# A hybrid attention and DeltaNet layer on one core: later transfers of weight sums, another queue for the reloads of y, and plain stores for the last results

## The chip, the core and the metric

The kernel runs on one core of a Trainium2 chip. A core has five engines with instruction lists of their own: TensorE (PE, matmuls; its weight loads are listed as PEld), VectorE (DVE), ScalarE (ACT), GpSimd (POOL) and SyncE (SP). They meet only at semaphores. Transfers between the chip's memory (DRAM) and the core's SBUF are issued from the list of SP or of GpSimd and are moved by 16 DMA engines. An engine works through its list in order, so what stands behind a waiting instruction waits too.

The metric is the device time of one execution in microseconds. Where a single execution is looked at, it is one that the profiler recorded.

## The reference, cut to what matters

One decoder layer for 512 positions (T) and width 2048 (D), all in float32:

```python
h = rms_norm(x, norm_w) * (1.0 + scale) + shift        # scale, shift, gate from c
proj = h @ w_in
y_a = (swa_attention(aq, ak, av, sinks) * silu(ag)) @ w_o_swa
o = gated_delta_rule(dq, dk, dv, g, beta)              # 32 heads, chunks of 64
y_b = (rms_norm(o, dn_norm_w) * silu(dz)) @ w_o_dn
y = sigmoid(mg_a) * y_a + sigmoid(mg_b) * y_b
return x + gate * (y @ w_out)
```

The change concerns the last line: `y @ w_out`, the gate, and the addition of x.

## The kernel before, in words

A float32 product is made of three matmuls on halves of a number: `split` (line 50) casts a tile to a high part on ACT (line 52, `whi`) and subtracts to get the low part on DVE (line 53, `wlo`), and `mm3` (line 237) issues the three matmuls, lines 240 to 242. Every weight tile of 1 MB is loaded by SP into one of two `raw` buffers (`load_job`, line 195), split in two halves into one of three pairs of `whi` and `wlo`, and used by PE. `channel_tile` (line 244) is one tile of 128 channels: 48 matmuls of 512 columns. After each second step of eight it calls `pump` (line 81), so 8 times a tile. `pump` does the weight work that is due, moves on the live chains of the heads, and moves on the side jobs in `self.side`: each has a rate, which is added at each pump, and takes one step whenever the sum reaches 1.

The stages, in order: startup; keys of the DeltaNet and a triangular solve; 16 head groups of five channel tiles each (`heads`, line 828: a query tile, two value tiles, two gate tiles), beside which the scan of the group runs as a live chain; the DeltaNet's output product (`branch_b`); attention; and `finish`.

*The sums.* The last product is a 2 x 2 block product in Strassen's manner with seven block products, m1 to m7 (`out_order`, line 1370). It needs sums of blocks of `w_out`. `weight_sums` (line 665) makes them by transfers alone, in DRAM: four copies of 1 MB from x to the output (line 670, one a step), and then for each of four parts of the blocks four copies by SP (line 683) and four accumulating transfers by GpSimd (line 687) of 1 MB each. It counts 4 + 4 x 12 = 52 steps. It is a side job `ws`, put beside the heads at line 643, ahead of group 0, with a rate of 0.15. `ordered` (line 657) ties every step's instructions behind the last matmul written so far.

*The last product.* In `finish` (line 1311) y is made in 16 tiles of 128 x 512, stored to the DRAM tensor `y_d` (line 1333), and its plain block forms (a11, a12, s3) are split at once. The other four forms (s1, s2, s4, a22) take the place of the activations `hh` and `hl`, which are used until the last tile of y. So they are made in `output` (line 1387), beside the product, by the generator `combos` (line 1345): 16 steps, one for each item of weights (half a tile, 12 matmuls). Each loads a pair of y tiles, `ya` and `yc`, by SP, into buffers with the tags `m` and `yb`, and computes on DVE and ACT. The tags `m` and `yb`, of two buffers each, are also those of y's own making and of results. `prep` (line 1395) splits the weights two items ahead. The raw tiles lie in the pool `fraw` of four buffers, and a new load (`out_load`, line 1376) is issued when a tile's second half is split.

*The results.* `evict` (line 1419) adds block products from PSUM as they are finished. `columns` (line 1413) multiplies by the gate and adds the result to the output, which holds x already, by an accumulating transfer from GpSimd (line 1417), 16 in all. The last two are m3's, at the kernel's end.

*The order.* Within an engine the order of instructions is not the order of the Python lines. It is fixed when the program is built, by a scheduler that goes by the program's order as a priority and by its own estimates of when inputs are there. Ties like `behind` (line 105) bind it.

Of the kernel before, what the change touches and what calls it, by code (L numbers as in the profile page):

```python
# [16 lines left out]
P = 128  # L17
T = 512
# [18 lines left out]
class Layer:  # L37
# [552 lines left out]
    def deltanet(self):  # L590
        tc, nc, a = self.tc, self.nc, self.a
        dram = self.dram
        self.lt_d = dram.tile([2, 2, 16, 4, HD, HD], F32, name="lt_d")
        self.lab_d = dram.tile([VH, HD, 4, HD], F32, name="lab_d")
        self.ta_d = dram.tile([2, 16, 4, HD, HD], F32, name="ta_d")
        self.ts_d = dram.tile([2, 2, 16, 4, HD, HD], F32, name="ts_d")
        self.kT_d = dram.tile([KH, P, T], F32, name="kT_d")
        self.k_d = dram.tile([KH, P, T], F32, name="k_d")
        self.o_d = dram.tile([VH, P, T], F32, name="o_d")
        self.ws_d = {k: dram.tile([P, 2048], F32, name=f"ws{k[0]}{k[1]}{k[2]}") for k in self.sum_keys()}  # L600
        with ExitStack() as ps:
            self.pmm = ps.enter_context(tc.tile_pool(name="pmm", bufs=2, space=PSUM, reuse_waits="tile"))
            self.ptp = ps.enter_context(tc.tile_pool(name="ptp", bufs=2, space=PSUM, reuse_waits="tile"))
            self.gwk = ps.enter_context(tc.tile_pool(name="gwk", bufs=1, reuse_waits="tile"))
            sol1 = ps.enter_context(tc.tile_pool(name="sol1", bufs=1, side="right", reuse_waits="tile"))
            with ExitStack() as sa:
                wk = sa.enter_context(tc.tile_pool(name="dnA", bufs=2, reuse_waits="tile"))
                sol0 = sa.enter_context(tc.tile_pool(name="sol0", bufs=1, reuse_waits="tile"))
                gp = sa.enter_context(tc.tile_pool(name="gates", bufs=1, reuse_waits="tile"))
                self.go(self.gates(gp), 1)  # L610
                self.keys_done, self.solve_in = [], {}
                self.keep_order = True
                for g in range(NST):
                    self.go(self.keys(wk, g, self.acc_k[g]), 10 + 8 * g)
                for j in range(NFIRST):
                    self.merge_gate("mb", j, self.mb_d)
                self.go(self.solve_load(sol0, 0), 1)
                self.go(self.solve_load(sol1, 1), 1)
                s0 = self.paced(self.solve(sol0, 0, nc.vector), 0.82)
                s1 = self.paced(self.solve(sol1, 1, nc.vector), 0.0)  # L620
                for kind, j in self.mixed():
                    if kind == "k":
                        self.go(self.keys(wk, j, self.channel_tile(f"k{j}")), 0)
                    else:
                        self.merge_gate("mb", j, self.mb_d)
                        if j == KT - 3:
                            s0[1] = 1.2
                for j in range(3):
                    self.merge_gate("ma", j, self.ma_d)
                    if s0 not in self.slow:  # L630
                        s1[1] = 1.1
                self.drain_live()
                self.drain_slow(s0)
                self.keep_order = False
                s1[1] = 0.6
            with ExitStack() as sb:
                wk = sb.enter_context(tc.tile_pool(name="dnB", bufs=2, reuse_waits="tile"))
# [12 lines left out]
                self.drain_live()  # L650
                self.drain("ws")
        self.dump("o", self.o_d)
# [658 lines left out]
    def finish(self):  # L1311
        tc, nc, a = self.tc, self.nc, self.a
        with ExitStack() as es:
# [31 lines left out]
    def combos(self, wk, A):  # L1345

        nc = self.nc
        lo, hi = slice(0, 256), slice(256, 512)
        TT = nc.vector.tensor_tensor
        for second in range(2):  # L1350
            for kt in range(8):
                p = wk.tile([P, T], F32, tag="m", name="ya")
                nc.sync.dma_start(out=p, in_=self.y_d[kt])
# [3 lines left out]
                TT(out=p[:, hi], in0=p[:, hi], in1=q[:, hi], op=ALU.subtract)  # L1357
                if second:
                    TT(out=p[:, lo], in0=p[:, hi], in1=p[:, lo], op=ALU.add)
                    TT(out=p[:, lo], in0=p[:, lo], in1=q[:, lo], op=ALU.subtract)  # L1360
                    self.split(A["a22"][0][:, kt, :], A["a22"][1][:, kt, :], q[:, hi])
                else:
                    nc.vector.scalar_tensor_tensor(
                        out=p[:, lo], in0=p[:, hi], scalar=-1.0, in1=p[:, lo], op0=ALU.mult, op1=ALU.subtract
                    )
                    self.split(A["s1"][0][:, kt, :], A["s1"][1][:, kt, :], p[:, hi])
                n = "s4" if second else "s2"
                self.split(A[n][0][:, kt, :], A[n][1][:, kt, :], p[:, lo])

    def out_order(self):  # L1370
        return [
# [15 lines left out]
    def output(self, es, wk, A):  # L1387
# [18 lines left out]
        side = self.combos(wk, A)  # L1406
        next(side, None)
        todo = []
        keep = {}
        ps = {}  # L1410
        gt = wk.tile([P, 2, T], F32, tag="gt", name="gt", bufs=1)

        def columns(n, c, t, src, sign):

            csl = slice(c * 1024 + n * T, c * 1024 + n * T + T)
            nc.vector.scalar_tensor_tensor(out=src, in0=src, scalar=sign, in1=gt[:, c, :], op0=ALU.mult, op1=ALU.mult)
            nc.gpsimd.dma_start(out=self.out[t * P : (t + 1) * P, csl], in_=src, accum_op=ALU.add)

        def evict(n, name):
            TT = nc.vector.tensor_tensor  # L1420
            for t in range(2):
                b = ps[name, t]
                if name == "m1":
                    o = t * 1024 + n * T
                    nc.sync.dma_start(out=gt[:, t, :], in_=self.gate_d[o : o + T].partition_broadcast(P))
# [21 lines left out]
                elif name == "m3":  # L1447
                    k = keep["m5", t]
                    TT(out=k, in0=b, in1=k, op=ALU.add)
                    columns(n, 1, t, k, -1.0)  # L1450

        for i in range(2):
            prep(i)
# [130 lines left out]
```

## Time and profile before

| what | us |
|---|---|
| median of 3 runs | 2952.16 (2951.74 to 2953.14) |
| the profiled execution | 2957.62 |
| its span, first to last instruction | 2955.9 |
| PE busy | 2880.3 |
| DVE busy | 1744.2 |
| ACT busy | 1085.7 |
| GpSimd busy | 232.7 |

Busy is the time in which an engine has an instruction in work. A window's row gives, for a stretch of the span, the busy time of PE, PEld, DVE, ACT and POOL with the count of their instructions, the clock granted to PE as a share of full, the busy share of the DMA engines, and GB/s. A timeline row gives start, duration, engine, line, operation, and in brackets the idle time ahead of it and what ended that. A row that starts with a line and `x16: a/b/c` has minimum, median and maximum in ns of that line's instructions, and the first and last start.

### The profile page before, as it was taken

Reading aid. Unit: us, or ns where it says so; the run is one execution under the profiler, and the core shown is the slowest. Engines: PE = TensorE matmul, PEld = TensorE weight load, DVE = VectorE, ACT = ScalarE, POOL = GpSimd, SP = SyncE. Lnnn points to the kernel's source line nnn. Section 1 sums busy time; section 2 is a strip of 40 time slices with the busy share of each in tenths; the row PEclk is TensorE's granted clock in tenths of the full one; section 3 lists DMA queues with packets and bytes.
Section 4 is the critical chain, followed back from the end, with each engine's and each line's share of the span. In section 5 each row is a group of like instructions: output and inputs, shape, how many; then the busy total and the mean of one; then the engine's idle time right before and its main releaser. Section 6 shows DMA issues by size and latency. Waiting matters only on the chain.

```text
span 2955.9 us, 38055 instructions
## 1 busy us (share of the span) xinstructions
PE 2880.3 (97%) x14556; PEld 2354.2 (80%) x14556; DVE 1744.2 (59%) x2883; ACT 1085.7 (37%) x2113; POOL 232.7 (8%) x220
## 2 busy tenths in 40 slices
PE   8899999899999999999999999999999999999988
PEld 6677888778888888888888778888788888888867
DVE  6765998667776545555444453433755655554575
ACT  4354334233334333333333322312344434432343
POOL 0022211011110101100000000000100000000000
PEclk9999999999999999999999999999999999999999
DMA  9747555656565854333332575554322232274575
GB/s 379 283 148 223 167 155 168 238 152 203 176 191 154 240 156 146 118 121 117 123 108 100 210 266 183 189 174 160 105 88 88 76 102 102 104 270 163 192 232 161
DMA packets 177415, 497.26 MB, mean 168 GB/s; under 512 B 72945, under 2 KB 75505, under 8 KB 137361
## 3 DMA queue, kind: packets, MB, share of 16 engines
q1 hardware_dynamic: 172626, 473.87, 47.4%
q0 software_dynamic: 4608, 20.97, 4.0%
q8 instruction: 114, 1.87, 0.3%
q14 instruction: 67, 0.55, 0.1%
HBM read 433.09 MB, written 97.20 MB: 179 GB/s over the span
## 4 chain that ended last, share of the span: by engine, by line
PE 71%; issue 16%; DMA 2%; DVE 2%; ACT 1%; POOL 1%; SPq 0%; POOLq 0%; DVEq 0%; ACTq 0%
PE mm L240 21%; PE mm L242 20%; PE mm L241 20%; PE pv L958 1%; PE po L977 1%; PE pp L948 1%; PE po L976 1%; PE S L1248 1%; PE pd L973 1%; DMA oraw<-o_d 1%; DMA qe<-eg_rows 1%; PE pP L274 1%; PE O L1299 1%; PE pqk L909 1%; PE ptv L274 0%
## 5 line engine op out<-in xcount | busy, mean ns | idle before, releaser
L240 PE MATMUL mm<-hh,whi 128*128 128x512 f32 x2784 | 1132.2, 407 | 9.3 <-ACT whi L52 8.5
L242 PE MATMUL mm<-hh,wlo 128*128 128x512 f32 x2784 | 1092.0, 392 | 2.9 <-DVE wlo L53 2.8
L241 PE MATMUL mm<-hl,whi 128*128 128x512 f32 x2784 | 1089.4, 391 | 0.0
L53 DVE TENSOR_TENSOR wlo<-raw,whi 128x1024 fp32r<-128x1024 f32 (+1 forms) x428 | 524.2, 1228 | 512.6 <-ACT whi L52 491.6
L52 ACT CAST whi<-raw 128x1024 fp32r<-128x1024 f32 (+1 forms) x428 | 444.9, 1043 | 935.9 <-PE mm L241 913.3
L240 PEld LDWEIGHTS mm<-hh,whi 128*128 128x128 f32 x2784 | 525.2, 189 | 120.4 <-ACT whi L52 10.3
L242 PEld LDWEIGHTS mm<-hh,wlo 128*128 128x128 f32 x2784 | 523.8, 188 | 119.2 <-DVE wlo L53 6.2
L241 PEld LDWEIGHTS mm<-hl,whi 128*128 128x128 f32 x2784 | 525.5, 189 | 99.1 <-issue 0.4
L240 PE MATMUL mm<-oh,whi 128*128 128x512 f32 x512 | 201.4, 395 | 1.6 <-ACT whi L52 0.9
L241 PE MATMUL mm<-ol,whi 128*128 128x512 f32 x512 | 199.9, 391 | 1.0 <-DVE ol L53 1.0
L242 PE MATMUL mm<-oh,wlo 128*128 128x512 f32 x512 | 199.9, 391 | 0.5 <-DVE wlo L53 0.5
L754 POOL TENSOR_TENSOR E<-E,neg_g 128x512 f32<-128x512 f32 x64 | 77.9, 1216 | 522.5 <-DMA E<-g_rows 382.0
L240 PEld LDWEIGHTS mm<-oh,whi 128*128 128x128 f32 x512 | 96.5, 189 | 24.2 <-ACT oh L52 2.0
L241 PEld LDWEIGHTS mm<-ol,whi 128*128 128x128 f32 x512 | 96.4, 188 | 22.8 <-DVE ol L53 2.0
L242 PEld LDWEIGHTS mm<-oh,wlo 128*128 128x128 f32 x512 | 96.5, 189 | 21.1 <-DVE wlo L53 1.2
L804 DVE TENSOR_TENSOR A<-A,atmp 128x62 f32<-128x62 f32 (+30 forms) x124 | 111.3, 898 | 1.6
L797 DVE TENSOR_TENSOR atmp<-A 128x62 f32<-128x62 f32 (+30 forms) x124 | 111.0, 895 | 1.5
L905 POOL TENSOR_TENSOR qe<-qe,yq 128x512 f32<-128x512 f32 x32 | 49.3, 1557 | 720.4 <-DMA qe<-eg_rows 604.2
L53 DVE TENSOR_TENSOR wlo<-raww,whi 128x1024 fp32r<-128x1024 f32 x56 | 68.2, 1222 | 26.9 <-ACT whi L52 26.9
L52 ACT CAST whi<-raww 128x1024 fp32r<-128x1024 f32 x56 | 58.6, 1051 | 58.3 <-PE m L242 46.8
L951 DVE SCALAR_TENSOR_TENSOR r<-pp,neg_eg,vt 128x128 f32<-128x128 f32 x96 | 29.3, 347 | 79.5 <-PE pp L948 78.3
L580 DVE SCALAR_TENSOR_TENSOR yv<-mm,convh,yv 128x511 f32<-128x511 f32 (+2 forms) x96 | 71.6, 745 | 5.2 <-ACT yv L576 3.5
(326 smaller groups left out, 3137.2 us busy)
## 6 DMA issues: line engine op xcount, KB each, us to landing
raw<-in_w_ch SPq DMA_DIRECT2D x158, 1024.0 KB
wa<-in_w_ada_ss SPq DMA_DIRECT2D x32, 1024.0 KB
raw<-in_w_od SPq DMA_DIRECT2D x32, 1024.0 KB
E<-g_rows SPq DMA_DIRECT2D x64, 256.0 KB
wsm<-in_w_out POOLq DMA_DIRECT2D x16, 1024.0 KB, 9.2
gw<-in_w_ada_gate SPq DMA_DIRECT2D x16, 1024.0 KB
raw<-in_w_os SPq DMA_DIRECT2D x16, 1024.0 KB
raww<-wsm SPq DMA_DIRECT2D x16, 1024.0 KB
```

Of the source, the lines that this page charges most:

```text
L52: self.nc.scalar.copy(out=hi, in_=src)
L53: self.nc.vector.tensor_tensor(out=lo, in0=src, in1=hi.bitcast(F32), op=ALU.subtract)
L240: nc.tensor.matmul(ps, lhsT=wh, rhs=xh, start=first, stop=False)
L241: nc.tensor.matmul(ps, lhsT=wh, rhs=xl, start=False, stop=False)
L242: self.last_mm = nc.tensor.matmul(ps, lhsT=wl, rhs=xh, start=False, stop=last).ins
L274: self.nc.tensor.transpose(dst[:, c * P : (c + 1) * P], src_cols(c), self.ident)
L580: nc.vector.scalar_tensor_tensor(out=y[:, s:], in0=ps[:, : T - s], scalar=w[:, j : j + 1], in1=y[:, s:], op0=ALU.mult, op1=ALU.add)
L754: nc.gpsimd.tensor_tensor(out=E, in0=E, in1=ng, op=ALU.add)
L797: eng.tensor_tensor(out=t, in0=A[:, m : m + 1, m + 1 :].to_broadcast([P, m, n]), in1=A[:, :m, m : m + 1].to_broadcast([P, m, n]), op=ALU.mult,
L804: eng.tensor_tensor(out=A[:, :m, m + 1 :], in0=A[:, :m, m + 1 :], in1=t, op=ALU.add)
L905: nc.gpsimd.tensor_tensor(out=qf, in0=qf, in1=q, op=ALU.mult)
L909: nc.tensor.matmul(pqk[:, c, :], lhsT=kT[:, sl(c)], rhs=q[:, sl(c)], start=True, stop=True)
```

## The change

Three parts of the kernel differ.

- `weight_sums` is put beside the heads at group 2, with a rate of 0.13.
- `combos` loads its pairs of y through GpSimd's queue, into two buffers each of the tags `ya` and `yc`. Steps 0 and 1 are loaded at the beginning, and step i + 2 when step i is done. `fraw` has three buffers instead of four, which is the same space.
- In the second half of the columns (n = 1), m3's two results get x by an addition on DVE, from a tile that SP loads at m4's eviction into the tag `yb`, and are stored by SP without accumulation.

```diff
-                self.beside(self.ordered(self.weight_sums()), 0.15, "ws")
                 for g in range(KH):
+                    if g == 2:
+                        self.beside(self.ordered(self.weight_sums()), 0.13, "ws")
...
-            self.wpool = es.enter_context(tc.tile_pool(name="fraw", bufs=4, reuse_waits="tile"))
-            for _ in range(4):
+            self.wpool = es.enter_context(tc.tile_pool(name="fraw", bufs=3, reuse_waits="tile"))
+            for _ in range(3):
                 self.out_load()
...
-                p = wk.tile([P, T], F32, tag="m", name="ya")
-                nc.sync.dma_start(out=p, in_=self.y_d[kt])
-                q = wk.tile([P, T], F32, tag="yb", name="yc")
-                nc.sync.dma_start(out=q, in_=self.y_d[kt + 8])
-                yield
...
+        steps = [(second, kt) for second in range(2) for kt in range(8)]
+        pairs = {}
+
+        def load(i):
+            if i < len(steps):
+                kt = steps[i][1]
+                for j, tag in enumerate(("ya", "yc")):
+                    t = wk.tile([P, T], F32, tag=tag, name=tag)
+                    nc.gpsimd.dma_start(out=t, in_=self.y_d[kt + 8 * j])
+                    pairs[i, j] = t
+
+        load(0)
+        load(1)
+        yield
+        for i, (second, kt) in enumerate(steps):
+            p, q = pairs.pop((i, 0)), pairs.pop((i, 1))
...
+            load(i + 2)
+            yield
...
-        def columns(n, c, t, src, sign):
+        def columns(n, c, t, src, sign, x=None):
...
-            nc.gpsimd.dma_start(out=self.out[t * P : (t + 1) * P, csl], in_=src, accum_op=ALU.add)
+            dst = self.out[t * P : (t + 1) * P, csl]
+            if x is None:
+                nc.gpsimd.dma_start(out=dst, in_=src, accum_op=ALU.add)
+            else:
+                nc.vector.tensor_tensor(out=src, in0=src, in1=x, op=ALU.add)
+                nc.sync.dma_start(out=dst, in_=src)
...
+                if (n, name) == (1, "m4"):
+                    last[t] = wk.tile([P, T], F32, tag="yb", name="x")
+                    nc.sync.dma_start(out=last[t], in_=a["x"][t * P : (t + 1) * P, 1024 + T : 2048])
...
-                    columns(n, 1, t, k, -1.0)
+                    columns(n, 1, t, k, -1.0, last.get(t) if n else None)
```

The arithmetic of a step in `combos` is the same.

More of the change, by code (lines that the diff above doesn't have):

```diff
@@ L1349, in combos @@
         TT = nc.vector.tensor_tensor
-        for second in range(2):
-            for kt in range(8):
-                p = wk.tile([P, T], F32, tag="m", name="ya")
-                nc.sync.dma_start(out=p, in_=self.y_d[kt])
-                q = wk.tile([P, T], F32, tag="yb", name="yc")
-                nc.sync.dma_start(out=q, in_=self.y_d[kt + 8])
-                yield
[L1357 to L1368, printed above, removed]
+        steps = [(second, kt) for second in range(2) for kt in range(8)]
@@ new lines, in combos @@
+        pairs = {}
[11 more added lines that the diff above has]
+            p, q = pairs.pop((i, 0)), pairs.pop((i, 1))
+            TT(out=p[:, hi], in0=p[:, hi], in1=q[:, hi], op=ALU.subtract)
+            if second:
+                TT(out=p[:, lo], in0=p[:, hi], in1=p[:, lo], op=ALU.add)
+                TT(out=p[:, lo], in0=p[:, lo], in1=q[:, lo], op=ALU.subtract)
+                self.split(A["a22"][0][:, kt, :], A["a22"][1][:, kt, :], q[:, hi])
+            else:
+                nc.vector.scalar_tensor_tensor(
+                    out=p[:, lo], in0=p[:, hi], scalar=-1.0, in1=p[:, lo], op0=ALU.mult, op1=ALU.subtract
+                )
+                self.split(A["s1"][0][:, kt, :], A["s1"][1][:, kt, :], p[:, hi])
+            n = "s4" if second else "s2"
+            self.split(A[n][0][:, kt, :], A[n][1][:, kt, :], p[:, lo])
+            load(i + 2)
+            yield
```

3 lines of the change are left out of this document (2 added, 1 removed).

## The prediction

> **What bounds the kernel now.** I read the page first (busy shares, the chain), then windows by stage to find where TensorE is not busy, then the timelines of those places and what each engine waited for there.
>
> ```profile
> span 2955.9 us, 38055 instructions
> PE 2880.3 (97%) x14556; PEld 2354.2 (80%) x14556; DVE 1744.2 (59%) x2883; ACT 1085.7 (37%) x2113; POOL 232.7 (8%) x220
> ```
>
> TensorE (PE) is busy for 2880.3 of 2955.9 us, so a change can win only where PE idles or runs at a lowered clock. Two such places, and the tail, are touched by the diff.
>
> The first is the start of the 16 head groups. A group ends its query tile with the scaled copy `yq` on ScalarE (ACT), so the distance of these rows is a group's length. The rows are those of groups 0 to 3 and of the fifteenth.
>
> ```profile
> 536.96 0.68 ACT L576 ACTIVATE yq<-mm,convh 128x512 f32<-128x512 f32 x1
> 615.43 0.69 ACT L576 ACTIVATE yq<-mm,convh 128x512 f32<-128x512 f32 x1 [2.37 <-PE mm L242]
> 692.63 0.68 ACT L576 ACTIVATE yq<-mm,convh 128x512 f32<-128x512 f32 x1
> 759.93 0.68 ACT L576 ACTIVATE yq<-mm,convh 128x512 f32<-128x512 f32 x1
> 1502.87 0.68 ACT L576 ACTIVATE yq<-mm,convh 128x512 f32<-128x512 f32 x1
> ```
>
> Groups 0 and 1 take 78.5 and 77.2 us, group 2 takes 67.3, and the eleven behind it (1502.87 - 759.93) / 11 = 67.5 each. So the first two hold 78.5 + 77.2 - 2 x 67.3 = 21.1 us more than their share. The windows (PE, PEld, DVE, ACT and POOL busy, granted clock, DMA share, GB/s) show that it is idle PE and, behind each gap, a lowered clock:
>
> ```profile
> 525.00:550.00 25.00, 25.00 (x114) 20.68 (x113) 20.88 (x31) 7.77 (x16) 3.42 (x4) 1.00 0.98 327
> 550.00:575.00 25.00, 20.17 (x82) 16.04 (x81) 18.63 (x24) 5.47 (x8) 2.73 (x3) 0.86 0.62 198
> 575.00:600.00 25.00, 20.38 (x117) 15.17 (x116) 10.46 (x18) 7.79 (x15) 1.84 (x2) 1.00 0.57 169
> 600.00:625.00 25.00, 20.69 (x100) 16.44 (x100) 15.79 (x38) 8.98 (x32) 0.00 (x0) 0.92 0.30 84
> 725.00:750.00 25.00, 25.00 (x136) 20.79 (x135) 18.16 (x26) 9.17 (x17) 1.67 (x2) 1.00 0.89 256
> ```
>
> PE loses 4.8, 4.6 and 4.3 us in three windows whose DMA share is only 0.62, 0.57 and 0.30, and nothing at 0.89. So bandwidth alone is not the loss. The timeline shows the order in which it comes about:
>
> ```profile
> 536.17 0.53 SPq L200 DMA_DIRECT2D raw<-in_w_ch  x1
> 562.10 0.63 ACT L585 ACTIVATE th<-yv 128x512 f32<-128x512 f32 x1 [2.45 <-DVE yv L580]
> 562.63 1.03 ACT L52 CAST whi<-raw 128x1024 fp32r<-128x1024 f32 x1
> 563.71 0.79 PE L240 MATMUL mm<-hh,whi 128*128 128x512 f32 x1 [4.79 <-ACT whi L52]
> ```
>
> The load of this weight tile was issued at 536.17, 26.5 us before its cast. The cast shows no wait of its own: it stands in ACT's list behind `th`, which waits for the tile that PE has just finished. PE idles 4.79 us for it. The list is fixed when the program is built, by a scheduler that reckons with transfers, and it is only so around the first transfers of the sums:
>
> ```profile
> L670 SPq DMA_DIRECT2D out<-in_x x4: 547/583/1657, 534.4 to 566.5; - x4
> L683 SPq DMA_DIRECT2D wsm<-in_w_out x8: 501/580/1135, 583.8 to 1003.0; - x8
> L687 POOL DMA_DIRECT2D wsm<-in_w_out x16: 807/842/1026, 592.4 to 1121.3; - x16
> L824 SPq DMA_DIRECT2D ts_d<-A x8: 445/592/2095, 526.9 to 998.1; - x8
> ```
>
> The four copies of x lie from 534.4 to 566.5, right behind the first solve's stores `ts_d` (from 526.9).
>
> The second place is the last product, 56 half weight tiles of 12 matmuls. Here are its first, seventh and last matmul, then its two halves as windows, one of its stalls in the timeline, and a row of the SP queue's waits (us in all, times, longest):
>
> ```profile
> 2779.06 0.39 PE L240 MATMUL m<-whi,a11h 128*128 128x512 f32 x1
> 2780.42 0.39 PE L240 MATMUL m<-whi,a11h 128*128 128x512 f32 x1
> 2945.47 0.39 PE L242 MATMUL m<-whi,hl 128*128 128x512 f32 x1
> ```
>
> ```profile
> 2779.00:2861.00 82.00, 73.31 (x306) 57.51 (x306) 58.90 (x101) 38.91 (x60) 1.77 (x2) 0.98 0.81 265
> 2861.00:2946.00 85.00, 84.42 (x369) 68.56 (x367) 56.63 (x66) 32.34 (x34) 10.41 (x12) 1.00 0.67 179
> ```
>
> ```profile
> 2827.77 0.43 DVE L1357 TENSOR_TENSOR ya<-ya,yc 128x256 f32<-128x256 f32 x1 [3.82 <-DMA ya<-y_d]
> 2829.04 1.22 DVE L53 TENSOR_TENSOR wlo<-raww,whi 128x1024 fp32r<-128x1024 f32 x1
> 2830.17 0.42 DVE L53 TENSOR_TENSOR hl<-ya,hh 128x256 fp32r<-128x256 f32 x1
> 2830.31 0.50 PE L241 MATMUL m<-wlo,hh 128*128 128x512 f32 x1 [1.18 <-DVE wlo L53]
> ```
>
> ```profile
> SPq L1353 <- DMA out<-c: 8.5, 2, 5.3
> ```
>
> Six matmuls take 1.36 us, so one takes 0.2267 and an item of twelve 2.72. The 672 take 671 x 0.2267 = 152.1 us from first start to last start, and took 166.4: 14.3 us are lost, nearly all in the first half. VectorE (DVE) waits for a `y` load, the weight split `wlo` stands behind it, and PE waits for `wlo`. Two loads waited together 8.5 us for an accumulating store of a result to land, because `ya` shares its two buffers with `c`.
>
> **The change part by part.**
>
> *Transfers of the sums two groups later, at 0.13 for 0.15.* The same 52 steps (4 of x, 48 of sums) are issued, with the same instructions. A group has 5 tiles of 8 pumps, so 52 / 0.13 = 400 pumps are ten groups: done in group 12 of 16. What can be had is 21.1 us. What can be lost again is the same order of stalls two groups later, so the bounds are a gain of 21.1 and, if the copies of x do there what they do now, 0, or a little below. Between: the sums go through groups 2 to 5 at 8 transfers in 12 steps, so 0.15 x 8 / 12 = 0.10 MB a pump, and cost nearly nothing (67.3 to 67.5 us a group); the copies of x went at 0.15 and stood beside 10.5 us lost a group. At 0.13 a straight line gives 6.3 us for a group, and the four steps last 31 pumps, 0.77 of a group: 5.0 us come back. I take 21.1 - 5.0 = 16.1. On the queues nothing new waits: SP's weight loads and GpSimd's mask additions stand behind these transfers as they did in groups 2 to 8.
>
> *The loads of y.* 32 issues leave SP, 32 come to GpSimd (POOL). Of SP's, nothing was on the path. POOL's issues, and how long its transfers took to land, are known only for accumulating stores:
>
> ```profile
> L1417 POOL DMA_DIRECT2D out<-c x8: 862/862/906, 2816.4 to 2935.0; - x8
> DMA to landing us min/median/max: 4.0/5.2/12.3
> 2870.00:2880.00 10.00, 9.56 (x41) 7.00 (x40) 10.00 (x14) 3.15 (x3) 3.48 (x4) 1.00 0.90 211
> L1357 DVE TENSOR_TENSOR ya<-ya,yc x16: 418/426/428, 2775.9 to 2857.4; 128x256 f32<-128x256 f32 x16
> ```
>
> So 32 x 0.862 = 27.6 us on an engine with 12.2 us of work in the stage: no bound. A load may go when step i has left its buffer and is needed at step i + 2. With two buffers a step can therefore not come faster than half of (its own 1.45 + second issue 0.86 + landing): 3.8 us at a landing of 5.2, and 7.3 at 12.3. Now the sixteen steps start from 2775.9 to 2857.4, 5.4 us apart. So loads at the median are early enough: 15 x 3.8 = 57 us, and the last step is first needed by the last item of m4, 23 x 2.72 = 63 us in. DVE itself: an instruction starts 0.09 before the one before has ended (2829.04 to 2830.17 is 1.13 for a 1.22 one), so a step of 4 or 5 with one `wlo` is 2.45 or 2.78 us beside PE's 2.72. That fits. The ten evictions of m6, at 0.60 each, are 6.0 us and exceed the lead of one item by 3.3; that stays, and so does the second half's 85.00 - 84.42 = 0.6. I take 14.3 - 3.9 = 10.4, with bounds of 14.3 and, for loads at 12.3, 15 x (7.3 - 5.4) = 28 us lost.
>
> A rule speaks against this part. The Trainium skill, "SBUF — State Buffer", in "SBUF: two separate sides", says that descriptors of GpSimd's transfers cannot be written while VectorE holds the port the two share. The window's row above speaks against its reach here: with DVE busy for 10.00 of 10, four issues cost POOL 3.48 us, 0.87 each. By the page the loads would be late and the time the third rival's 2962; by the row it is 2924.
>
> *Weight buffers 4 to 3.* A tile serves two items and its buffer is loaded anew five items before need, 13.6 us instead of 19.0. The nearest landing of 1 MB is that of the accumulating sums:
>
> ```profile
> DMA to landing us min/median/max: 8.2/9.2/14.0
> ```
>
> That is 9.2 in the median and 14.0 at most. I cost it at nothing; the cover is those 13.6 us, and without it every tile would hold the casts by its lateness. One 1 MB load fewer stands ahead of the first tiles of this stage, worth less than 1 us and left out.
>
> *The last two results.* Two additions of x and two stores by SP replace two accumulating stores. The two loads of x go out at m4's eviction, four items or 10.9 us ahead of need, which hides them. The timeline of the end, and of a plain store and the load that waits for its buffer:
>
> ```profile
> 2945.22 1.37 DVE L1449 TENSOR_TENSOR m<-m,m 128x512 f32<-128x512 f32 x2 [4.71 <-PE m L242]
> 2946.51 1.28 DVE L1416 SCALAR_TENSOR_TENSOR m<-m,gt 128x512 f32<-128x512 f32 x2
> 2947.48 1.75 POOL L1417 DMA_DIRECT2D out<-m  x2 [6.67 <-DVE m L1416]
> ```
>
> ```profile
> 2758.94 0.32 SPq L1333 DMA_DIRECT2D y_d<-m  x1
> 2761.01 0.32 SPq L1327 DMA_DIRECT2D m<-ma_d  x1
> ```
>
> Now: second issue at 2948.35, landing 4.0 to 5.2 later, 2952.4 to 2953.6. Then: six DVE instructions at 0.64 from 2945.22 end at 2949.1; a store of this size frees its buffer for the next load within 2.07 us, so 2951.2. That is 1.2 to 2.4 us gained, and a loss of up to 1.0 if the plain store took 4.0. I take 2.0, as the plain store's own row is nearer.
>
> *Sum.* 16.1 + 10.4 + 2.0 = 28.5 us. The profiled execution took 2957.62 us (span 2955.9), 5.5 above the median of the runs; the sum is made within it and taken from the median: 2952.16 - 28.5 = 2923.7, rounded 2924. The ceilings 21.1 + 14.3 + 2.4 = 37.8 give 2914.
>
> **The rivals.** (1) *The stall travels.* The copies of x make the scheduler put the casts late wherever they are, and groups 2 and 3 lose the 21.1. For it: the same four copies and the same first pair of sums follow each other. Against: a lower rate, and no `ts_d` stores just ahead. Then 12.4 remain: 2940.
>
> (2) *The y loads were not what held the stage.* DVE and its order are, and its gain is 0: 2952.16 - 18.1 = 2934. For it: DVE's 58.90 us in the first half are already 72%. Against: it stood idle for `ya` ahead of the splits. The Trainium skill, "DMA: Bandwidth & Descriptors", in "Issuing engines are not separate DMA queues", says that another issuing engine saves only issue time; by that alone this rival would hold. The 8.5 us for a shared buffer are a thing that page does not speak of.
>
> (3) *Slower: y lands late.* GpSimd's loads land like its slowest store, 12.3 us after issue, a step comes every 7.3 us and the stage loses 28 more: 2952.16 - 16.1 - 2.0 + 28 = 2962. It decides against the change from where the stage loses 18.1: 5.4 + 18.1 / 15 = 6.6 us a step, a landing of 10.9. For it: the 12.3 was seen. Against: the median of 5.2.
>
> (4) *It does not do what it says*: (1) and (2) at once, 2950.
>
> **How the numbers follow.** Forecast 0.56 (its own range 2914 to 2935), (1) 0.16, (2) 0.09, (3) 0.13, (4) 0.06. About 0.2%, 5.9 us, is what a measurement of this kernel can tell from no change. Faster: 0.56 + 0.16 + 0.09 = 0.81; same 0.06; slower 0.13. The range runs from 2912, a little under the ceilings' sum, to 2948, which leaves out (3) and (4), 0.19.
>
> **What would show it.** `yq` of groups 0 and 1 some 67 us apart and PE at 25.00 in each window to 625; groups 2 and 3 at most 5 us longer than 67.3 in sum. In the last product no `ya` wait ahead of a `wlo`, the sixteen steps done within about 60 us, and 156 us from first to last matmul. At the end two stores by SP, and 2 us less from the last matmul to the end of the span. Wrong are: casts in pairs in groups 2 and 3 (rival 1); DVE waits on `ya` of over 2 us (rival 3); PE waiting for `wlo` with DVE never idle (rival 2).

## The result, and the profile after

The changed kernel takes 2955.7 us in the median of 14 runs (2950.42 to 2960.46), the kernel before, run beside it, 2953.58 us (14 runs, 2949.02 to 2960.62). The ratio is 1.0005 with a 95% interval of 0.9997 to 1.0014: no change that can be measured, where 28.5 us less were forecast. The profiled execution took 2958.95 us, 3.3 above its median.

The head of the page after:

```profile
span 2956.1 us, 38061 instructions
PE 2884.4 (98%) x14556; PEld 2359.3 (80%) x14556; DVE 1750.1 (59%) x2885; ACT 1084.5 (37%) x2113; POOL 250.7 (8%) x250
```

**Head groups.** The timeline of ACT in the changed kernel: the `yq` copies of groups 0 to 4.

```profile
537.20 0.68 ACT L576 ACTIVATE yq<-mm,convh 128x512 f32<-128x512 f32 x1
600.33 0.68 ACT L576 ACTIVATE yq<-mm,convh 128x512 f32<-128x512 f32 x1
668.48 0.68 ACT L576 ACTIVATE yq<-mm,convh 128x512 f32<-128x512 f32 x1
759.27 0.69 ACT L576 ACTIVATE yq<-mm,convh 128x512 f32<-128x512 f32 x1 [16.46 <-PE mm L242]
835.72 0.68 ACT L576 ACTIVATE yq<-mm,convh 128x512 f32<-128x512 f32 x1
```

Groups 0 and 1 now take 63.1 and 68.2 us (78.5 and 77.2 before): 24.4 us won. Groups 2 and 3 take 90.8 and 76.5 (67.3 and 68.3 before): 31.7 us lost. The stall has moved two groups on and grown by 7.

The windows over groups 0 and 1, and over groups 2 and 3, of the kernel before:

```profile
536.96:692.63 155.67, 140.85 (x684) 113.13 (x683) 102.97 (x159) 48.62 (x105) 20.71 (x19) 0.95 0.61 190
692.63:828.20 135.57, 134.77 (x715) 111.98 (x714) 100.48 (x160) 50.18 (x114) 16.90 (x16) 1.00 0.59 180
```

and of the changed one:

```profile
537.20:668.48 131.28, 130.63 (x684) 108.28 (x683) 100.57 (x159) 48.61 (x104) 17.99 (x16) 1.00 0.45 147
668.48:835.72 167.24, 150.04 (x715) 120.43 (x714) 102.48 (x160) 49.89 (x114) 17.24 (x15) 0.90 0.49 152
```

The two rows of 684 matmuls are the same work with and without the stall, and so are the two of 715. In groups 0 and 1 the stall cost 14.8 - 0.65 = 14.2 us of idle PE (span less busy) and 140.85 - 130.63 = 10.2 us in which the same matmuls ran longer, at a mean clock of 0.95. In groups 2 and 3 it costs 17.2 - 0.8 = 16.4 us idle and 150.04 - 134.77 = 15.3 us at a clock of 0.90. More than half of the growth is the lower clock. Two windows of group 2 show how it comes about:

```profile
707.43:714.25 6.82, 4.34 (x22) 3.10 (x22) 2.00 (x7) 2.87 (x9) 0.00 (x0) 1.00 0.00 0
714.25:721.07 6.82, 5.84 (x14) 4.07 (x15) 5.78 (x8) 2.23 (x4) 0.00 (x0) 0.50 0.23 82
```

PE is idle for 2.48 us of the first, in gaps of at most 0.98 us, and the clock of the second is 0.50. The Trainium skill, "TensorE: Matmul & The Clock Gate", in "HAM oscillation — how this bites in real kernels", describes a kernel whose clock is throttled again and again behind waits between short stretches of matmuls, and gives the rule that no gap of idle PE should exceed about 3.4 us. The trace agrees that the clock falls behind such waits, and not that a gap must be that long: here gaps of 0.98 us, close together, were enough. A single gap does not always do it either: the 2.20 us ahead of 581.06 in the kernel before left the clock at 1.00 (the row from 575 to 600 in the prediction).

The DMA share is 0.49, lower than the 0.59 of the undisturbed groups 2 and 3 of before: bandwidth is not what is missing.

ACT and PE of the changed kernel in group 2:

```profile
740.83 1.98 ACT L52 CAST whi<-raw 128x1024 fp32r<-128x1024 f32 x2
741.92 0.79 PE L240 MATMUL mm<-hh,whi 128*128 128x512 f32 x1 [2.06 <-ACT whi L52]
```

Casts stand in pairs, with no wait for a DMA of their own, and PE waits for them. This is the sign that the prediction named for its first rival. Casts are not all that PE waits for in groups 2 and 3: 2.06 us fall to this cast and 13.8 to instructions of VectorE. The experiments below remove both together.

**Last product.** First and last matmul, and the two halves as windows:

```profile
2782.87 0.39 PE L240 MATMUL m<-whi,a11h 128*128 128x512 f32 x1
2949.34 0.39 PE L242 MATMUL m<-whi,hl 128*128 128x512 f32 x1
```

```profile
2783.00:2865.00 82.00, 73.36 (x300) 58.38 (x299) 59.80 (x99) 36.19 (x54) 14.86 (x25) 0.94 0.74 240
2865.00:2949.30 84.30, 84.30 (x373) 69.81 (x372) 51.03 (x56) 32.73 (x33) 8.66 (x10) 1.00 0.70 202
```

The product takes 166.5 us, as before (166.4), where 156 were forecast. The second half lost its 0.4 us of idle PE; the first has as much idle time as before and a lower clock (0.94 for 0.98). One of its stalls, in the timeline of POOL, DVE and PE:

```profile
2790.95 1.21 POOL L1359 DMA_DIRECT2D ya<-y_d  x2 [1.54 <-DVE hl L53]
2797.02 0.43 DVE L1367 TENSOR_TENSOR ya<-ya,yc 128x256 f32<-128x256 f32 x1 [4.56 <-DMA ya<-y_d]
2797.74 0.54 POOL L1359 DMA_DIRECT2D yc<-y_d  x1 [5.58 <-DVE ya L1367]
2799.43 0.50 PE L241 MATMUL m<-wlo,a12h 128*128 128x512 f32 x1 [2.56 <-DVE wlo L53]
```

GpSimd could issue `ya` only when `hl` had left its buffer (2790.95). DVE is ready for it 1.5 us later, waits 4.56 us, and the weight split behind it is late for PE. The buffer of the next `yc` is freed by the very instruction that waited, so that load goes out behind the wait too. The loads are two steps ahead in the program and hardly ahead on the chip.

**The end.**

```profile
2949.09 1.37 DVE L1469 TENSOR_TENSOR m<-m,m 128x512 f32<-128x512 f32 x2 [4.74 <-PE m L242]
2951.57 1.29 DVE L1433 TENSOR_TENSOR m<-m,x 128x512 f32<-128x512 f32 x2
2952.29 0.95 SPq L1434 DMA_DIRECT2D out<-m  x2
```

From the last matmul (2949.34) to the end of the span (2956.1) it takes 6.8 us; before it took 2955.9 - 2945.47 = 10.4. So 3.6 us are won. The changed kernel began the last product 3.8 us behind the kernel before (2782.87 against 2779.06), the product took as long, and these 3.6 us pay the lag back.

### The profile page after: what moved, and what is told of

It is laid out like the page before. It is cut to its first block, busy times and chain, and to the rows that moved or that the text cites. A ratio compares the mean times of both kernels' runs of the same rounds, so it can differ in the third digit from the quotient of the medians.

```text
span 2956.1 us, 38061 instructions
## 1 busy us (share of the span) xinstructions
PE 2884.4 (98%) x14556; PEld 2359.3 (80%) x14556; DVE 1750.1 (59%) x2885; ACT 1084.5 (37%) x2113; POOL 250.7 (8%) x250
## 4 chain that ended last, share of the span: by engine, by line
PE 86%; DMA 2%; DVE 2%; issue 1%; ACT 1%; POOL 0%; SPq 0%; DVEq 0%; POOLq 0%; ACTq 0%
PE mm L240 24%; PE mm L242 24%; PE mm L241 24%; PE m L241 1%; PE m L242 1%; PE m L240 1%; PE S L1249 1%; PE pv L959 1%; PE po L978 1%; PE O L1300 1%; PE pP L274 1%; PE pd L974 1%; PE po L977 1%; PE pp L949 1%; DMA ya<-y_d 1%
## 5 line engine op out<-in xcount | busy, mean ns | idle before, releaser
L52 ACT CAST whi<-raww 128x1024 fp32r<-128x1024 f32 x56 | 58.8, 1052 | 62.1 <-PE m L242 54.4
```

Source lines behind the costliest of these rows:

```text
L52: self.nc.scalar.copy(out=hi, in_=src)
```

## The experiments

The theories at the start. A: the stall goes with the transfers, wherever they begin; which of them, and whether the list or the chip, is to be found. C: the loads of y are still late, or were not the cause. Each timed run is compared with runs of the kernel before on the same chip.

### The first part alone

```diff
-                self.beside(self.ordered(self.weight_sums()), 0.15, "ws")
                 for g in range(KH):
+                    if g == 2:
+                        self.beside(self.ordered(self.weight_sums()), 0.13, "ws")
```

> The kernel before with the transfers of x and of the sums moved to group 2 at 0.13, and nothing else. Theory A (the stall goes with these transfers, whatever group they start in): groups 0 and 1 at 63 to 68 us, groups 2 and 3 together some 32 us over 2 x 67.3, the distance from the first to the fifth yq about 298 us against 291 before, and a time 4 to 9 us above before. Theory B (in the changed kernel the late groups are hurt by the other two edits, not by this one): the distance of the first five yq near 275 us and a time some 16 us below before.

Measured: 2957.01 us against 2954.47, ratio 1.0013 (1.0004 to 1.0022). Its `yq` rows of groups 0, 2 and 4:

```profile
536.88 0.68 ACT L576 ACTIVATE yq<-mm,convh 128x512 f32<-128x512 f32 x1
668.17 0.68 ACT L576 ACTIVATE yq<-mm,convh 128x512 f32<-128x512 f32 x1
835.27 0.68 ACT L576 ACTIVATE yq<-mm,convh 128x512 f32<-128x512 f32 x1
```

131.3 and 167.1 us, 298.4 in all: the changed kernel's numbers, from this part alone. Theory B is out.

### Copies of x and sums apart

```diff
                 for g in range(KH):
+                    if g == 0:
+                        self.beside(self.ordered(self.x_copies()), 0.15, "xc")
+                    if g == 2:
+                        self.beside(self.ordered(self.weight_sums()), 0.13, "ws")
```

`x_copies` is the first loop of `weight_sums`, taken out of it.

> The kernel before with weight_sums cut in two: the four copies of x start in group 0 at 0.15 as before, the 48 transfers of sums in group 2 at 0.13. Theory A1 (the copies of x make the scheduler put the weight casts late): groups 0 and 1 keep 76 to 80 us each, groups 2 and 3 take 67 to 69, time within 5 us of before. Theory A2 (the first pair of sums does it): groups 0 and 1 at 67, groups 2 and 3 some 20 to 30 us over. Theory A3 (the long steps of the second solve on DVE make late casts dear in groups 2 and 3): with the sums alone there, at least 10 us over in groups 2 and 3 whatever the x copies do.

Measured: 2953.83 against 2954.47, ratio 0.9998 (0.9989 to 1.0007). The same three rows:

```profile
539.33 0.68 ACT L576 ACTIVATE yq<-mm,convh 128x512 f32<-128x512 f32 x1
695.16 0.68 ACT L576 ACTIVATE yq<-mm,convh 128x512 f32<-128x512 f32 x1
830.71 0.68 ACT L576 ACTIVATE yq<-mm,convh 128x512 f32<-128x512 f32 x1
```

Groups 0 and 1 keep their stall (155.8 us), groups 2 and 3 have none (135.6) though all 48 steps of the sums now begin there. It is the four copies of x, and neither the sums nor the second solve's long DVE steps. What the changed kernel moved was the copies.

### Copies of x far away

```diff
+            self.beside(self.ordered(self.x_copies()), 0.05, "xc")
             for n in range(4):
                 self.group(wk, kd[n], n, blk, mask, sink, qw)
```

This is in the attention stage; the sums start in group 0 at 0.15.

> The kernel before with the four copies of x taken out of the head groups and made during the attention stage (0.05 a pump), the sums in group 0 at 0.15 as before. Theory A1 (copies of x): groups 0 and 1 at 67 to 70 us, the distance of the first five yq 270 to 276 us, time 14 to 21 us below before, as the attention stage has a DMA share of 0.27 and PE at 100.00 of 100 to hide them in. Theory A2 (first pair of sums): groups 0 and 1 stay above 75 and the time stays within 5 us of before. If the stall only goes where the copies go, the attention stage grows by some 20 us and the time is as before.

Measured: 2964.11 against 2954.47, ratio 1.0032 (1.002 to 1.0045), so slower and not as before; its profiled execution, 2959.2, is the shortest of its five. The head groups are nearly free, 270.5 us from the first to the fifth `yq`:

```profile
535.75 0.68 ACT L576 ACTIVATE yq<-mm,convh 128x512 f32<-128x512 f32 x1
806.22 0.68 ACT L576 ACTIVATE yq<-mm,convh 128x512 f32<-128x512 f32 x1
```

and the attention stage, where the copies were issued from 2091.72 to 2186.69, pays. Two windows and a row of ACT:

```profile
2100.00:2150.00 50.00, 45.28 (x241) 35.09 (x240) 21.68 (x52) 14.32 (x31) 2.75 (x2) 0.93 0.26 94
2200.00:2250.00 50.00, 43.45 (x246) 34.63 (x245) 32.18 (x72) 18.47 (x46) 4.60 (x3) 0.90 0.24 80
2116.93 2.93 ACT L52 CAST whi<-raw 128x1024 fp32r<-128x1024 f32 x3
```

Before, both windows had PE at 50.00 and a clock of 1.00; now it idles for 4.7 and 6.6 us. The lead of 21.4 us that this kernel has at its last `yq` (1548.76 against 1570.18) is a lag of 4.1 when the last product begins (2783.11 against 2779.06). At DMA shares of 0.26 and 0.24 there is little to contend for; three casts stand side by side. The stall goes wherever the copies go, as the last sentence of the expectation had it; its price of some 20 us was low, as 25.5 are lost here.

### The same copies, cut into rows

How can a copy between two places in memory hold ACT's casts? Not by holding up the weights: in the trace of the kernel before, the last packets of the two weight loads issued at 536.17 and 543.78 end at 544.8 and 552.7, and the cast that PE waits for starts at 562.63. Here is the order in which ACT's instructions of one group ran in the traces (Q, V, Z: the first copy of a query, value or gate tile; C: a weight cast; a dot: anything else but the reading of an accumulator), of the kernel before, of the changed one, and of one in which the copies have one more argument:

```
before, group 1     Q............CCCCCV...C.CVC....CZ..C...C.Z....C.C
changed, group 2    Q....C........CV.C.V.......CCZ.Z............CC
changed, group 3    Q.....CCCCCV...C.CVC....CZ..C...C.Z....C.C
x in rows, group 1  Q....C........CV...C.CVC..CZ..C...C.Z....C.C
```

```diff
-            nc.sync.dma_start(out=self.out[s], in_=self.a["x"][s])
+            nc.sync.dma_start(out=self.out[s], in_=self.a["x"][s], max_dma_last_dim=8192)
```

> The kernel before with one argument more: the four copies of x keep their queue, place and rate, but are cut into 128 rows of 8 KB (max_dma_last_dim=8192, which the accumulating transfers of the sums have already) where they now go as 16 runs of 64 KB. In the program as built ACT's casts then stand one by one in groups 0 and 1, no longer in twos to fives. Theory L (what costs the time is the order in ACT's fixed list, which the scheduler chose by its own reckoning of these copies): the first five yq 269 to 276 us apart against 291, PE busy in all windows from 525 to 625, and a time 15 to 21 us below before. Theory M (the chip itself is slowed by 4 MB more in this place, whatever the list): the distance stays at 285 or above and the time within 5 us of before.

Measured: 2932.97 against 2953.6, ratio 0.9924 (0.9912 to 0.9937), 20.6 us less. First and fifth `yq`, and the window of groups 0 and 1:

```profile
539.36 0.68 ACT L576 ACTIVATE yq<-mm,convh 128x512 f32<-128x512 f32 x1
807.05 0.68 ACT L576 ACTIVATE yq<-mm,convh 128x512 f32<-128x512 f32 x1
539.36:671.47 132.11, 131.29 (x684) 108.32 (x683) 100.60 (x159) 48.59 (x104) 21.01 (x19) 1.00 0.71 225
```

267.7 us, PE at 131.29 of 132.11, the clock at 1.00, with all the transfers in their old place and a DMA share of 0.71, above the 0.61 of the stalled kernel. Theory M is out: the chip carries these 4 MB there, in rows, without harm.

### The same copies, uncut, by another queue

```diff
-            nc.sync.dma_start(out=self.out[s], in_=self.a["x"][s])
+            nc.gpsimd.dma_start(out=self.out[s], in_=self.a["x"][s])
```

with the sums started late as in the changed kernel.

> The sums late as in e1 (group 2, 0.13, the copies of x uncut in 16 runs of 64 KB), but the four copies of x are issued by GpSimd and not by SyncE. In the program as built the casts of groups 2 and 3 then stand one by one. Theory L (ACT's list): no stall in any group, the first five yq 269 to 276 us apart against 298 in e1, time 15 to 21 us below before. Theory M' (runs of 64 KB hold up the weight loads on the chip): groups 2 and 3 stay 20 to 32 us over and the time is that of e1, 3 us above before.

Measured: 2929.26 against 2953.6, ratio 0.9914 (0.9901 to 0.9928), 24.3 us less. First and fifth `yq`:

```profile
536.45 0.68 ACT L576 ACTIVATE yq<-mm,convh 128x512 f32<-128x512 f32 x1
803.53 0.68 ACT L576 ACTIVATE yq<-mm,convh 128x512 f32<-128x512 f32 x1
```

267.1 us, with the copies still in 16 runs of 64 KB, and ACT's order in groups 2 and 3 has no casts side by side:

```
group 2    Q....C........CV.C.CV.C.CZ..C...C.Z....C.C
group 3    Q....C........CV.C.CV.C.CZ.....C....C.Z....C.C
```

Theory M' is out too. Whether the copies are cut or whole, early or late, the time follows the order of ACT's list. Why the scheduler sets it so is not shown. That it reckons an uncut copy on SyncE's queue as a long one, and so believes the weight loads behind it late, would fit these runs, but it does not explain one thing: the 16 copies of the sums that SP issues (line 683) go in 16 runs of 64 KB as well, and when they began in group 2 with the copies of x left in group 0, no cast was late.

### The loads of y alone, and a square of queue by depth

The second part alone:

```diff
-                p = wk.tile([P, T], F32, tag="m", name="ya")
-                nc.sync.dma_start(out=p, in_=self.y_d[kt])
+                    t = wk.tile([P, T], F32, tag=tag, name=tag)
+                    nc.gpsimd.dma_start(out=t, in_=self.y_d[kt + 8 * j])
```

> The kernel before with the loads of y alone changed (GpSimd's queue, own buffers, two steps ahead, three weight buffers). The prediction's theory (a late load in a shared buffer holds VectorE): first to last matmul of the last product 156 us against 166.4, time 10 us below before. Theory C (the order of VectorE's list is what holds the weight splits, and the loads still wait for a buffer that was left late): 163 to 167 us, VectorE still waiting on ya for 2 us or more at several places, time within 4 us of before.

Buffers for four steps in the weight buffers that lie idle by then, loads by SyncE:

```diff
+                t = self.wraw.tile([P, 2048], F32, tag="raw", name="yr")
+                for e in range(2):
+                    for j in range(2):
+                        u = t[:, (2 * e + j) * T : (2 * e + j + 1) * T]
+                        nc.sync.dma_start(out=u, in_=self.y_d[steps[i + e][1] + 8 * j])
```

> The kernel before with the y loads on SyncE into buffers of their own that hold four steps (the two 8 KB weight buffers of the earlier stages, idle by then), so each load is issued four steps ahead; four 8 KB weight buffers stay. Theory D (late loads hold VectorE, and two steps ahead on GpSimd's queue was not enough): VectorE waits less than 2 us in all on y, first to last matmul 156 to 159 us, time 7 to 10 us below before. Theory O (the order of VectorE's list is what counts: steps that are ready stand ahead of the weight splits): VectorE no longer waits on y, but PE still waits for wlo behind steps, 161 us or more, time at most 5 us below before.

The second part with SyncE (`nc.sync` for `nc.gpsimd`), and the four-step buffers with GpSimd (`nc.gpsimd` for `nc.sync`):

> e5 (own buffers for two steps, loads two steps ahead, three weight buffers) with the loads issued by SyncE in place of GpSimd. With e5, e9 and e11 it makes a square of queue by depth. Theory Q (it is GpSimd's queue that brings the loads late): first to last matmul 156 to 159 us as in e9, against 167 in e5. Theory N (two steps are too few, whichever queue: a load is issued only when the step two before has left its buffer): 162 us or more, VectorE waiting on ya for 8 us or more in all.

> e9 (own buffers for four steps) with the loads issued by GpSimd. Theory Q: 162 us or more from first to last matmul and less than half of e9's gain of 9 us. Theory N: 156 to 159 us, time 6 to 10 us below before, so depth alone would have made the change's second part work.

Measured, with the length from first to last matmul of the last product (166.4 before), PE's idle time in it and the clock of its first 82 us:

| loads of y | length | PE idle | clock | DVE's waits for y in it: sum, longest | ratio to before (95%) |
|---|---|---|---|---|---|
| before: shared buffers, SyncE | 166.4 | 9.0 | 0.98 | 20.6, 3.8 | |
| two steps, GpSimd | 167.0 | 8.3 | 0.94 | 11.3, 4.2 | 1.0011 (1.0002 to 1.002) |
| four steps, GpSimd | 170.9 | 12.0 | 0.92 | 15.8, 7.4 | 1.0023 (1.0013 to 1.0033) |
| two steps, SyncE | 157.7 | 3.9 | 1.00 | 12.5, 4.0 | 0.9975 (0.9965 to 0.9986) |
| four steps, SyncE | 156.1 | 2.7 | 1.00 | 7.6, 1.8 | 0.9968 (0.9955 to 0.998) |

The second part alone gave what its theory C expected. In the square the lengths and the times are those of theory Q: the queue makes a difference of 9 to 15 us, the depth 1.6 on SyncE, and on GpSimd more depth makes it worse. How much one execution says: in six kernels of this study that leave the y loads as before, the length was 161.1 to 166.2, and 166.4 before itself. Both GpSimd rows lie above that, both SyncE rows below; the 1.6 is inside such a spread. So the 14.3 us that the prediction found lost was a high draw, too.

The waits are not those of theory Q. With two steps DVE waits as long for y on SyncE as on GpSimd, so neither the sum nor the longest wait tells these two apart, and theory N's sign of 8 us or more is there on both. With four steps on SyncE it still waits 7.6 us, where theory D had less than 2. What differs is what PE feels. The first 82 us of the product, with two steps on GpSimd and on SyncE:

```profile
2779.00:2861.00 82.00, 73.67 (x298) 58.74 (x297) 59.41 (x100) 36.48 (x54) 15.35 (x26) 0.94 0.72 236
2776.00:2858.00 82.00, 78.08 (x339) 62.79 (x338) 65.85 (x106) 40.21 (x58) 5.26 (x6) 1.00 0.81 259
```

Of the 9.3 us between the two lengths, 4.4 are idle PE and the rest are matmuls that ran longer at the lower clock. GpSimd's row has less idle PE than the kernel before and is no shorter: three stalls of 2.2 to 2.6 us each in place of many short ones, and the clock goes to 0.94.

The queue also changes the order that the scheduler gives VectorE's list. Behind the first weight split of the stage, five or more instructions of the steps stand between two weight splits five times with two steps on GpSimd, and once on SyncE. No run has the one without the other, so it is open how much of the 9 to 15 us is the later arrival of GpSimd's loads and how much is this order.

The longest wait is that of four steps on GpSimd. Here it is, in the timelines of POOL, DVE and PE, with windows of the stretch:

```profile
2811.10 0.91 POOL L1430 DMA_DIRECT2D out<-c  x1 [10.02 <-DVE c L1429]
2812.46 0.42 DVE L53 TENSOR_TENSOR hl<-yr,hh 128x256 fp32r<-128x256 f32 x1
2812.84 0.88 POOL L1430 DMA_DIRECT2D out<-c  x1 [0.83 <-DVE c L1429]
2813.45 2.46 POOL L1359 DMA_DIRECT2D yr<-y_d  x4
2825.18 0.42 DVE L1367 TENSOR_TENSOR yr<-yr 128x256 f32<-128x256 f32 x1 [7.35 <-DMA yr<-y_d]
2826.51 0.80 PE L240 MATMUL m<-whi,hh 128*128 128x512 f32 x1 [6.29 <-ACT whi L52]
```

```profile
2813.00:2818.00 5.00, 5.00 (x23) 4.13 (x22) 4.83 (x10) 0.41 (x1) 2.92 (x5) 1.00 1.05 150
2818.00:2825.00 7.00, 2.22 (x10) 1.50 (x8) 0.00 (x0) 0.00 (x0) 0.00 (x0) 0.83 0.75 273
```

```profile
DMA to landing us min/median/max: 2.8/5.3/11.1
```

The last row is the landing of all 32 loads of this kernel. GpSimd stood 10.02 us at an accumulating store, waiting for DVE to finish its operand, but that is not what held the last four loads of y: the instruction that frees their buffer, the `hl` at 2812.46, ends at 2812.88, and the first of them is issued at 2813.45. The stores ahead cost them 0.6 us at most. Ahead of that `hl` in DVE's list stand two evictions, from 2808.92 on. Then the four loads take 8.05, 11.07, 11.00 and 11.11 us to land, DVE waits 7.35 us, a weight cast stands behind the same load in ACT's list, and PE waits 6.29 us for that. For such a landing the prediction had weighed the Trainium skill's "SBUF: two separate sides" ("SBUF — State Buffer"), which lets VectorE hold up GpSimd's descriptors. These rows do not decide on it: DVE was busy for 4.83 of 5.00 us while the four were issued, at 0.81 to 0.84 us each for the 0.54 of most others, and it was idle from 2818 to 2825, when none of the four had landed before 2821.50. What made them slow there, that, the two accumulating stores just ahead or something else, stays open.

### The end alone

```diff
+                nc.vector.tensor_tensor(out=src, in0=src, in1=x, op=ALU.add)
+                nc.sync.dma_start(out=dst, in_=src)
```

for the last two results, with the loads of x at m4.

> The kernel before with the last two results stored plainly and nothing else. From the last matmul's start to the end of the span 6.8 us as in the changed kernel, against 10.4 before; time 3 to 4 us below before. If the two loads of x or the added instructions cost anything in the product, its length from first to last matmul rises over 166.4 by that.

Measured: 2950.67 against 2953.6, ratio 0.9988 (0.9979 to 0.9997). Last matmul and last stores:

```profile
2936.72 0.39 PE L242 MATMUL m<-whi,hl 128*128 128x512 f32 x1
2939.66 0.95 SPq L1422 DMA_DIRECT2D out<-m  x2
```

The span ends at 2943.4, 6.7 us behind the last matmul: 3.7 us won. The product took 161.5 us here, 4.9 less than before, within the spread named above; its length shows no cost of the added loads and instructions.

### All three, mended

The copies of x on GpSimd with late sums, y four steps ahead on SyncE, the plain stores at the end:

> The three parts as the runs so far would have them: sums late with the copies of x on GpSimd's queue (e7), y four steps ahead on SyncE (e9), the last two results stored plainly (e8). If the three gains lie in different places and add, 24 + 9 + 3 = 36 us below before, 2917 us; if the chip gives part of it back (a lower clock, other waits), 2920 to 2930.

Measured: 2917.41 against 2952.94, ratio 0.9879 (0.9865 to 0.9892): 35.5 us less, where the three gains (24.3, 8.8 and 2.9 in the medians) add to 36.0. They lie in different places and add. Its windows over the head groups and over the product's two parts:

```profile
500.00:850.00 350.00, 348.81 (x1811) 289.29 (x1810) 260.42 (x399) 134.91 (x276) 43.17 (x42) 1.00 0.55 171
2751.00:2833.00 82.00, 79.98 (x349) 64.87 (x349) 66.64 (x106) 39.95 (x56) 5.97 (x7) 1.00 0.83 266
2833.00:2906.00 73.00, 73.00 (x324) 60.45 (x323) 41.95 (x45) 28.52 (x29) 6.20 (x8) 1.00 0.63 177
```

PE is idle for 3.2 us in 505, and the clock is full in all three. In the last product the sixteen steps can still be held behind the matmuls of their item:

```diff
-                    next(side, None)
+                    if p:
+                        with self.behind():
+                            next(side, None)
```

> e12 with the sixteen steps of the last product held behind the matmuls of their item and spread over three items in four, so that VectorE's list no longer has up to twelve step instructions ahead of a weight split. Theory O (the rest of the product's loss over 152.1 is this order): 153 to 155 us from first to last matmul, time 1 to 3 us below e12. Otherwise, if the rest is the evictions and the clock, 156 us as in e9; and if steps held back come late for a22 and s4, 158 or more.

Measured: 2915.54 against 2952.94, ratio 0.9873 (0.986 to 0.9887); 154.0 us from first to last matmul against 155.3, and DVE's waits for y in it fall from 6.2 to 0.3 us. The length is as theory O expects; the difference of 1.9 us in the times is inside both intervals. Its median is the lowest of all versions, 37 us below before.

## Why the prediction was wrong

**Sums two groups later (16.1 forecast; 7.3 lost in groups 0 to 3).** That 21.1 us could be had was right, and low (24.4). The step that failed is "at 0.13 a straight line gives 6.3 us for a group ... 5.0 us come back": 31.7 came back. The line joined the copies' rate to the loss, as if transfers cost time by their number; the loss is that of an instruction list that each uncut copy of x disorders, at a rate of 0.05 (25.5 us in the attention stage) as much as at 0.15. The case for the first rival was in the prediction (the same four copies follow each other; low DMA share in the stalled windows; the load issued 26.5 us before its cast), and it should have had the larger chance. Its price of zero was low too: it left out that the same stall costs more where it lowers the clock further.

**Loads of y (10.4 forecast; nothing).** That the stage can take 156 us was right: it takes 156.1 with loads by SyncE four steps ahead, and 154.0 where DVE's waits for y are 0.3 us. The step that failed is "So loads at the median are early enough". It compared mean paces, and the pace was not what failed: the steps of the changed kernel come 4.8 us apart (5.4 before), the last begins 58.8 us into the product, where 63 were allowed, and GpSimd's loads land in 4.3 us at the median, where 5.2 were taken. But PE is held by single waits, not by the pace. DVE's list takes the steps in pairs, so that two buffers come free together and the next pair is wanted at once: `ya` was issued at 2790.95, DVE was ready for it at 2792.46, and it landed at 2796.89, with a weight split behind. The third rival had lateness as its mechanism and a DVE wait of over 2 us as its sign, and the sign came; its price, 28 us from the slowest landing, did not: two steps on GpSimd cost 3 us over before by the ratio, four steps 7.

**Weight buffers 4 to 3 (nothing forecast).** Two steps on SyncE have three buffers, four steps have four. Their lengths, 157.7 and 156.1 us, differ by less than the spread between executions, so no cost shows; no run changes the buffers alone.

**The last two results (2.0 forecast; 3.6 in the span).** Right, and low. The plain stores came out nearly as reckoned: DVE is done at 2952.86, 3.77 us after its start, for 3.9, and in the trace SP sees the second store landed at 2955.16, 2.3 later, for 2.07. The mis-sized term is the end of the accumulating stores: the second landed at 2953.74, just above the 2952.4 to 2953.6 that were taken, and the span ended only 2.1 us behind that landing, as GpSimd's closing instruction lasts until 2955.10; behind the plain store's landing it ended after 0.9 us. The sum had no term for this.

**The sum.** By the ratios, part one costs 3.8 us, part two 3.2, and part three gains 3.5; the changed kernel's 1.0005 is what these make within their intervals. That it came out as no change is two losses and a gain that nearly cancel by chance. Rival 4's 2950 lies nearest to the measured time, and it is right on the stall and, by the SyncE runs, wrong on the loads of y.

## What to carry to other kernels

Before a transfer is moved, ask whether it costs time on the chip or disorders an engine's fixed list. Low DMA share, loads that landed long before use, and casts that show no wait of their own said here that it was the list; then moving the copies in time moved the stall with them, and a change in their form or queue removed it. Before a load is given more buffers, try it from another queue, and judge it by the single waits that PE feels, not by the mean pace. And a stall is priced as idle time and as the clock that it takes from the matmuls behind it: here 14.2 us idle cost 10.2 more, and 16.4 cost 15.3.

## What the runs showed that was not expected

- One argument on four copies (128 rows of 8 KB in place of 16 runs of 64 KB), with nothing moved, gained 20.6 us; the same copies issued in a stage where PE had never been idle, at DMA shares of 0.26 and 0.24, lost 25.5 us, more than the 20.8 that the head groups got back.
- The engine that issues a load mattered more than the depth of its buffers: 167.0 and 170.9 us on GpSimd, 157.7 and 156.1 on SyncE. The Trainium skill, "DMA: Bandwidth & Descriptors", in "Issuing engines are not separate DMA queues", says that issuing from several engines saves issue time only; here the other engine lost 9 to 15 us, with the order of VectorE's list changed along with it.
- Few long stalls were dearer than many short ones, by a little: with two steps on GpSimd 8.3 us of idle PE at a clock of 0.94 made the product as long as 9.0 us at 0.98 had before.
